# Three layer norms: the first token group finished from PSUM as the second one is, and the first tile's mean taken in a product bank

## The chip, the cores and the metric

The kernel runs on one core of a Trainium2 chip. The metric is device time in microseconds (us) of one execution; the time before is a median of three runs. The engines are named as in the profile: PE is TensorE, DVE is VectorE, ACT is ScalarE, POOL is GpSimd, SP issues the transfers. Each engine works its own queue strictly in order.

## The reference

Two trunk layers of a decoder run over 576 tokens (512 of a prompt, 64 of a sample), with D_MODEL = 1024. What matters here:

```python
def layer_norm(x, g, b):
    mu = jnp.mean(xf, -1, keepdims=True)
    var = jnp.mean(jnp.square(xf - mu), -1, keepdims=True)
    return ((xf - mu) * lax.rsqrt(var + LN_EPS)).astype(x.dtype) * g + b
...
        if l % 2 == 0:
            y, s1, wk1, r1 = ab_mixer(x, ...)
        else:
            y, c1 = conv_mixer(x, st_conv[i], w_in_conv[i], conv_w[i], w_out_conv[i])
        x = layer_norm(ALPHA * x + y, ln1_g[l], ln1_b[l])
        x = layer_norm(ALPHA * x + sqrelu_mlp(x, w_up[l], w_down[l]), ln2_g[l], ln2_b[l])
```

So there are four norms: norm 0 behind the first mixer, norm 1 behind the first MLP, norm 2 behind the conv mixer, norm 3 behind the second MLP, whose result is an output. The change is in the last three.

## The kernel before

**Layout.** Features lie on the partitions: x is eight tiles x0 to x7 of 128 features by 576 tokens. Tokens are cut into two groups, g0 and g1, of 288. A product of one feature tile and one group accumulates in one PSUM bank of the pool for products (`acc`, 6 banks); sums and means have a pool of two banks (`misc`). Weights and activations are each split into a high and a low part of a shorter format (`wh`, `wl`; `hh0` and `hl0` to `hh7` and `hl7` for the eight hidden tiles; `he`, `le`, `ho`, `lo` and again `hh`, `hl` for tiles of x), so each of the eight feature tiles of a contraction takes three matmuls (L152): high by high, low by high, high by low weight, and one product takes 24. The casts are L77 on ACT (high part) and L78 on DVE (low part).

**Norms 1 to 3.** A product that ends a residual branch is added to x tile by tile: `ln_add` (L271) for tile m = 0 to 7 and each group. At m = 0 the tile is added (L280; at norm 2, where the addition scales x too, L278), a matmul with a constant matrix takes its column mean into a bank named `cps` (L282), ACT copies it (L284), and it is taken off all eight tiles, on GpSimd at norms 1 and 3 (L291), on DVE at norm 2 (L289, L291). Tiles 1 to 7 are added by L293; ACT squares each (L296). Sums of the tiles and of their squares gather on GpSimd and DVE (L309) into `ln` and end in PSUM banks `ps` and `pq` by matmuls with constants (L319): all eight in one such sum for g0; for g1 tiles 6 and 7 go to the matmul directly.

**The finish.** When tile 7 of a group is added, the mean (`ps`) and mean square (`pq`) become a mean and a scale, and each tile is normalized, scaled and split for the next product. For g1 that is `ln_end` (L349), which keeps both in PSUM and works in place: d (L354), L355, Ln and Exp on ACT (L357, L358), the mean off each tile (L359, eight), L361 to L363, scale (L368, eight), high part on ACT (L375), low part on DVE (L376), x itself on ACT (L377). For g0 it is the other part of `ln_finish` (L380): mean and scale are copied to SBUF, five of the eight multiplications by the scale (L406) are on GpSimd.

**Order.** In the last product of a branch (`tail=TL`, 5) tiles 0 to 2 are done for both groups in turn, then tiles 3 to 7 of g0, then those of g1: g0's finish runs while PE works on g1's last five tiles. The code gives no order between engines; the framework's scheduler simulates a timeline and from it fixes each engine's queue before the run. Thus bank pools and buffers decide what stands where in PE's queue. The last tiles that norms 1 and 3 wait for are hh6, hl6, hh7, hl7, made from `ta` and `tb` in the branch before (ACT L1743, L1744, casts L77, L78). Behind norm 2 GpSimd forms sums of tiles of x (`ts`, L1712) and sums of weight tiles (L123, `raw`).

Of the kernel before, what the change touches and what calls it, by code (L numbers as in the profile page):

```python
# [10 lines left out]
F32 = mybir.dt.float32  # L11
F32R = mybir.dt.float32r
AF = mybir.ActivationFunctionType
ALU = mybir.AluOpType
PSUM = bass.MemoryType.PSUM

P = 128
NT = 576
GN = 288
KT = 8  # L20
ALPHA = 4.0 ** 0.25
LN_EPS = 1e-5


class Trunk:
# [245 lines left out]
    def ln_add(self, st, m, g, r, a, first):  # L271

        nc, cf = self.nc, self.cfg[st['n'], g]
        V, G = nc.vector, nc.gpsimd
        st[g, m] = r
        if m == 0:
            if first:
                V.scalar_tensor_tensor(out=r, in0=r, scalar=ALPHA, in1=a, op0=ALU.mult, op1=ALU.add)  # L278
            else:
                V.tensor_tensor(out=r, in0=r, in1=a, op=ALU.add)  # L280
            ps = self.p_misc.tile([P, GN], F32, tag="misc", name="cps")
            nc.tensor.matmul(ps, lhsT=self.ones128, rhs=r, start=True, stop=True)  # L282
            c = self.ln_tile(st, g, 'c')
            nc.scalar.copy(c, ps)  # L284
            for x in range(KT):
                t = st['x'][x][:, g * GN:(g + 1) * GN]
                e = G if x in cf['pg'] else V
                if first and x:
                    V.scalar_tensor_tensor(out=t, in0=t, scalar=ALPHA, in1=c, op0=ALU.mult, op1=ALU.subtract)  # L289
                else:  # L290
                    e.tensor_tensor(out=t, in0=t, in1=c, op=ALU.subtract)  # L291
        else:
            V.tensor_tensor(out=r, in0=r, in1=a, op=ALU.add)  # L293
        self.ln_sum(st, 's', m, g, r, cf['ds'], cf['sv'])
        t = self.p_tmp.tile([P, GN], F32, tag="t", name="lt", bufs=self.tb)
        nc.scalar.activation(t, r, AF.Square)  # L296
        self.ln_sum(st, 'q', m, g, t, cf['dq'], cf['qv'])
# [48 lines left out]
            nc.scalar.activation(r, r, AF.Identity, bias=b)  # L346
            if g and m == self.gated - 2: self.gate = [x.ins, y.ins]

    def ln_end(self, st, par, out, last):  # L349

        nc, V, pt = self.nc, self.nc.vector, self.p_tmp
        mean, v = st[1, 's', 'ps'], st[1, 'q', 'ps']
        d, w0, w = [pt.tile([P, GN], F32, tag="t", name=n, bufs=self.tb) for n in ('d', 'w0', 'w')]
        nc.scalar.activation(d, mean, AF.Square)  # L354
        V.scalar_tensor_tensor(out=v, in0=v, scalar=LN_EPS, in1=d, op0=ALU.add, op1=ALU.subtract)  # L355
        with self.tc.issue_after(self.pre.ins):
            nc.scalar.activation(w0, v, AF.Ln)  # L357
        nc.scalar.activation(w, w0, AF.Exp, scale=-0.5)  # L358
        sub = lambda r: V.tensor_tensor(out=r, in0=r, in1=mean, op=ALU.subtract)  # L359
        for m in range(3): sub(st[1, m])  # L360
        V.scalar_tensor_tensor(out=w0, in0=w, scalar=-0.5, in1=w, op0=ALU.mult, op1=ALU.mult)  # L361
        V.tensor_tensor(out=v, in0=v, in1=w0, op=ALU.mult)
        V.scalar_tensor_tensor(out=v, in0=v, scalar=1.5, in1=w, op0=ALU.add, op1=ALU.mult)  # L363
        gam, bet = par
        for m in range(KT):
            r, b = st[1, m], bet[:, m:m + 1]
            if m > 2: sub(r)
            V.scalar_tensor_tensor(out=r, in0=r, scalar=gam[:, m:m + 1], in1=v, op0=ALU.mult, op1=ALU.mult)  # L368
            if last:
                if m in (3, 6): V.tensor_scalar(out=r, in0=r, scalar1=b, scalar2=None, op0=ALU.add)  # L370
                else: nc.scalar.activation(r, r, AF.Identity, bias=b)
                out(m, 1, r)
                continue
            hi, lo = out(m, 1)
            x = nc.scalar.activation(hi, r, AF.Identity, bias=b)  # L375
            y = V.scalar_tensor_tensor(out=lo, in0=r, scalar=b, in1=hi.bitcast(F32), op0=ALU.add, op1=ALU.subtract)  # L376
            nc.scalar.activation(r, r, AF.Identity, bias=b)  # L377
            if m == self.gated - 2: self.gate = [x.ins, y.ins]

    def ln_finish(self, st, g, par, out, last=False):  # L380
        if g: return self.ln_end(st, par, out, last)
        nc = self.nc
        pt = self.p_tmp
        mean, e2 = st[g, 's', 'ps'], st[g, 'q', 'ps']
        mn = self.ln_tile(st, g, 'mn')
        nc.scalar.copy(mn, mean)
        d = pt.tile([P, GN], F32, tag="t", name="d", bufs=self.tb)
        nc.scalar.activation(d, mean, AF.Square)
        v = self.ln_tile(st, g, 'v')
        nc.vector.scalar_tensor_tensor(out=v, in0=e2, scalar=LN_EPS, in1=d, op0=ALU.add, op1=ALU.subtract)  # L390
        w0 = pt.tile([P, GN], F32, tag="t", name="w0", bufs=self.tb)
        with self.tc.issue_after(self.pre.ins):
            nc.scalar.activation(w0, v, AF.Ln)
        w = pt.tile([P, GN], F32, tag="t", name="w", bufs=self.tb)
        y = nc.scalar.activation(w, w0, AF.Exp, scale=-0.5)
        nc.vector.tensor_tensor(out=w0, in0=w, in1=w, op=ALU.mult)
        nc.vector.scalar_tensor_tensor(out=v, in0=v, scalar=-0.5, in1=w0, op0=ALU.mult, op1=ALU.mult)
        z = nc.vector.scalar_tensor_tensor(out=v, in0=v, scalar=1.5, in1=w, op0=ALU.add, op1=ALU.mult)
        if self.gated == 1 and g: self.gate = [z.ins, y.ins]
        gam, bet = par  # L400
        cf = self.cfg[st['n'], g]
        for m in range(KT):
            r = st[g, m]
            u = pt.tile([P, GN], F32, tag="t", name="u", bufs=self.tb)
            nc.vector.tensor_tensor(out=u, in0=r, in1=mn, op=ALU.subtract)  # L405
            (nc.vector if m in cf['mulv'] else nc.gpsimd).tensor_tensor(out=u, in0=u, in1=v, op=ALU.mult)  # L406
            def affine(e, o):
                if e is nc.scalar:
                    return e.activation(o, u, AF.Identity, scale=gam[:, m:m + 1], bias=bet[:, m:m + 1])
                return e.tensor_scalar(out=o, in0=u, scalar1=gam[:, m:m + 1], scalar2=bet[:, m:m + 1], op0=ALU.mult, op1=ALU.add)  # L410
            if last:
                affine(nc.vector if m in cf['affv'] else nc.scalar, r)
                out(m, g, r)
            else:
                dst = out(m, g)
                if self.direct:
                    a = affine(nc.scalar, dst[0])
                    affine(nc.vector, r)
                    b = nc.vector.tensor_tensor(out=dst[1], in0=r, in1=dst[0].bitcast(F32), op=ALU.subtract)
                    self.last = [a.ins, b.ins]  # L420
                else:
                    affine(nc.scalar, r)
                    self.parts(*dst, r)
            if self.gated >= 2 and g and m == self.gated - 2: self.gate = [x for x in self.last]


I32 = mybir.dt.int32
# [1437 lines left out]
```

## Time and profile before

| | |
|---|---|
| runs | 1532.83, 1533.28, 1534.14 us; median 1533.28 us |
| profiled execution | 1534.75 us, of which the traced span is 1533.0 us |
| PE, matmuls | 1465.6 us busy, 96% of the span |
| DVE | 1043.6 us, 68% |
| ACT | 647.4 us, 42% |
| GpSimd | 495.0 us, 32% |
| mean granted TensorE clock | 0.985 |

Times in rows of the trace are from the span's start. A row gives start, duration, engine, line, operation, tile written and tiles read, and in brackets how long the engine was idle before it and which engine's work ended that. The durations of matmuls overlap: at full clock one starts every 0.133 us though each shows 0.3 us. "x2" behind a row says that two like instructions are told together.

### The profile page before, as it was taken

The numbers are of one execution on the slowest core, as the hardware profiler recorded it, in microseconds if no ns is written. First come the engines' busy times: TensorE is split into PE (matmuls) and PEld (weight loads), VectorE is DVE, ScalarE is ACT, GpSimd is POOL, SyncE is SP. The second block draws the span as 40 slices with busy tenths as digits, with TensorE's granted clock in tenths as the row PEclk, the third lists the DMA queues.
The fourth block names the chain that finished last, engine by engine and source line by source line (L and its number), as shares of the span: only waits on it lengthen the run. The fifth ranks groups of instructions, "written<-read, shape, count | busy, mean of one in ns | idle before, by whom it ended". The sixth has DMA issues, their size and how long they took to land. (4 is left out here: it accounts for less than half of the span.)

```text
span 1533.0 us, 29786 instructions
## 1 busy us (share of the span) xinstructions
PE 1465.6 (96%) x11812; PEld 1416.3 (92%) x11812; DVE 1043.6 (68%) x2019; ACT 647.4 (42%) x1365; POOL 495.0 (32%) x554
## 2 busy tenths in 40 slices
PE   6999999999998999999999999899998999999996
PEld 5998898988787989999999998899998999999996
DVE  3565675876766984755747769788799475574755
ACT  3433433233333851533515435444366253351533
POOL 2032203356542331312213556332544131121354
PEclk9999999999999999999999999999999999999998
DMA  5332333535313042231422402223303223132221
GB/s 165 94 110 85 98 98 111 161 118 168 94 59 106 1 124 69 83 111 56 124 70 84 139 14 69 70 95 115 109 1 124 70 84 110 56 124 69 84 69 63
DMA packets 70940, 140.04 MB, mean 91 GB/s; under 512 B 21488, under 2 KB 30944, under 8 KB 70800
## 3 DMA queue, kind: packets, MB, share of 16 engines
q1 hardware_dynamic: 67968, 129.69, 27.3%
q0 software_dynamic: 1536, 5.57, 1.1%
q10 hardware_dynamic: 1296, 2.86, 0.6%
q8 instruction: 93, 1.52, 0.4%
q14 instruction: 47, 0.39, 0.1%
HBM read 124.39 MB, written 13.70 MB: 90 GB/s over the span
## 5 line engine op out<-in xcount | busy, mean ns | idle before, releaser
L77 ACT CAST wh<-raw 128x512 fp32r<-128x512 f32 x440 | 252.7, 618 | 409.1 <-PE acc L152 276.3
L78 DVE TENSOR_TENSOR wl<-raw,wh 128x512 fp32r<-128x512 f32 x440 | 325.9, 773 | 50.9 <-ACT wh L77 44.0
L152 PE MATMUL acc<-hh,wl 128*128 128x288 f32 x1180 | 348.7, 297 | 0.0
L152 PE MATMUL acc<-hl,wh 128*128 128x288 f32 x1180 | 348.1, 296 | 0.0
L152 PE MATMUL acc<-hh,wh 128*128 128x288 f32 x1180 | 345.7, 297 | 0.0
L152 PEld LDWEIGHTS acc<-hl,wh 128*128 128x128 f32 x1180 | 221.7, 188 | 0.5
L152 PEld LDWEIGHTS acc<-hh,wl 128*128 128x128 f32 x1180 | 221.6, 188 | 0.5
L152 PEld LDWEIGHTS acc<-hh,wh 128*128 128x128 f32 x1180 | 220.6, 188 | 0.3
L152 PE MATMUL acc<-xh,wh 128*128 128x288 f32 x480 | 148.3, 310 | 16.3 <-ACT xh L1541 13.3
L152 PE MATMUL acc<-ht,wh 128*128 128x288 f32 x444 | 133.0, 301 | 14.5 <-ACT s L244 6.1
L152 PE MATMUL acc<-xl,wh 128*128 128x288 f32 x480 | 146.2, 305 | 0.0
L152 PE MATMUL acc<-xh,wl 128*128 128x288 f32 x480 | 146.1, 304 | 0.0
L123 POOL TENSOR_TENSOR s<-raw 128x512 f32<-128x512 f32 x37 | 52.7, 1423 | 281.5 <-DMA raw<-in_w 210.8
L152 PE MATMUL acc<-lt,wh 128*128 128x288 f32 x444 | 132.4, 299 | 3.8 <-DVE lt L78 3.8
L152 PE MATMUL acc<-ht,wl 128*128 128x288 f32 x444 | 131.7, 298 | 0.0
L123 POOL TENSOR_TENSOR raw<-raw 128x512 f32<-128x512 f32 x37 | 57.2, 1545 | 164.2 <-DVE raw L123 110.0
L152 PEld LDWEIGHTS acc<-xh,wh 128*128 128x128 f32 x480 | 91.4, 191 | 19.8 <-ACT xh L1541 13.7
L152 PE MATMUL acc<-ho,wh 128*128 128x288 f32 x352 | 104.9, 298 | 0.0
L152 PE MATMUL acc<-lo,wh 128*128 128x288 f32 x352 | 104.5, 298 | 0.0
L152 PE MATMUL acc<-ho,wl 128*128 128x288 f32 x352 | 104.0, 298 | 0.0
L152 PEld LDWEIGHTS acc<-ht,wh 128*128 128x128 f32 x444 | 85.0, 192 | 16.4 <-ACT s L244 6.4
L152 PEld LDWEIGHTS acc<-xl,wh 128*128 128x128 f32 x480 | 91.5, 191 | 2.5 <-DVE xl L1542 0.7
(516 smaller groups left out, 3409.3 us busy)
## 6 DMA issues: line engine op xcount, KB each, us to landing
raw<-in_w SPq DMA_DIRECT2D x160, 512.0 KB, 3.8
raw<-in_w SPq DMA_DIRECT2D x60, 256.0 KB, 2.9
la<-in_w SPq DMA_DIRECT2D x32, 128.0 KB, 2.4
A<-stg SPq DMA_DIRECT2D x9, 288.0 KB, 3.2
x<-in_x POOLq DMA_DIRECT2D x8, 288.0 KB, 7.4
out_y<-x SPq DMA_DIRECT2D x16, 144.0 KB, 1.8
kr<-A SPq DMA_DIRECT2D x6, 288.0 KB, 2.6
lr<-in_x ACTq DMA_DIRECT2D x4, 288.0 KB
```

Source lines behind the costliest of these rows:

```text
L77: a = self.nc.scalar.copy(hi[:, s], src[:, s])
L78: b = self.nc.vector.tensor_tensor(out=lo[:, s], in0=src[:, s], in1=hi[:, s].bitcast(F32), op=ALU.subtract)
L123: tt = lambda e, o, x, y, op: e.tensor_tensor(out=o, in0=x, in1=y, op=op)
L152: mm = lambda w, x, a, b: self.nc.tensor.matmul(acc, lhsT=w, rhs=x, start=a, stop=b, skip_group_check=onto)
```

## The change

The column mean of m = 0 (`cps`) takes a bank of the product pool, for both groups of the three norms. `ln_end` becomes the only finish, for g0 too; the other part is gone. The copy of the mean, the multiplications on GpSimd and on DVE into `u`, and the temporary tiles go; for g0 there come eight L359, eight L368, eight L375, L376 and L377 (at norm 3 the last two kinds are replaced by the affine end). Behind the changed place the lines of the new kernel have smaller numbers: L1712 becomes L1666.

```diff
-            ps = self.p_misc.tile([P, GN], F32, tag="misc", name="cps")
+            ps = self.p_acc.tile([P, GN], F32, tag="acc", name="cps")
...
-    def ln_end(self, st, par, out, last):
+    def ln_finish(self, st, g, par, out, last=False):
...
-        mean, v = st[1, 's', 'ps'], st[1, 'q', 'ps']
+        mean, v = st[g, 's', 'ps'], st[g, 'q', 'ps']
...
-        for m in range(3): sub(st[1, m])
+        for m in range(3): sub(st[g, m])
...
-    def ln_finish(self, st, g, par, out, last=False):
-        if g: return self.ln_end(st, par, out, last)
...
-        mn = self.ln_tile(st, g, 'mn')
-        nc.scalar.copy(mn, mean)
...
-            nc.vector.tensor_tensor(out=u, in0=r, in1=mn, op=ALU.subtract)
-            (nc.vector if m in cf['mulv'] else nc.gpsimd).tensor_tensor(out=u, in0=u, in1=v, op=ALU.mult)
...
-                    affine(nc.scalar, r)
-                    self.parts(*dst, r)
```

The order of the queues moves at the following places. PE at norm 1, before: `acc_10122` is the product of m = 0, g0; `acc_10162` that of m = 0, g1; `acc_10210` and `acc_10241` those of m = 1.

```order
L152 MATMUL acc_10162<-hl3_6065,wh_9984 128x288
L152 MATMUL acc_10122<-hh6_6070,wh_9984 128x288
L152 MATMUL acc_10162<-hh3_6064,wl_9985 128x288
...
L152 MATMUL acc_10210<-hh1_6060,wh_9994 128x288
L152 MATMUL acc_10122<-hl6_6071,wh_9984 128x288
...
L152 MATMUL acc_10210<-hh4_6066,wh_9994 128x288
L152 MATMUL acc_10122<-hl7_6073,wh_9984 128x288
...
L152 MATMUL acc_10241<-hl3_6065,wh_9994 128x288
L282 MATMUL cps_10148<-x0_4548,o2_6036 128x288
L152 MATMUL acc_10241<-hh3_6064,wl_9995 128x288
L282 MATMUL cps_10188<-x0_4548,o2_6036 128x288
```

The same place now:

```order
L152 MATMUL acc_10122<-hh5_6068,wl_9985 128x288
L152 MATMUL acc_10122<-hh6_6070,wh_9984 128x288
L152 MATMUL acc_10122<-hl6_6071,wh_9984 128x288
L152 MATMUL acc_10122<-hh6_6070,wl_9985 128x288
L152 MATMUL acc_10122<-hh7_6072,wh_9984 128x288
L152 MATMUL acc_10122<-hl7_6073,wh_9984 128x288
L152 MATMUL acc_10122<-hh7_6072,wl_9985 128x288
L282 MATMUL cps_10148<-x0_4548,o2_6036 128x288
L152 MATMUL acc_10162<-hh0_6058,wh_9984 128x288
...
L152 MATMUL acc_10162<-hh7_6072,wl_9985 128x288
L282 MATMUL cps_10188<-x0_4548,o2_6036 128x288
```

The other products' matmuls no longer stand between those of the first product, and each mean stands directly behind its own product. It is so at norms 2 and 3 too; at norm 2 twelve matmuls of another sum (`acc<-ht`, `lt`) stand between hh5 and hh6, ahead of them 18 of the first product now and 24 matmuls before.

ACT at norm 2, before (`ta` and `tb` become hh6 and hh7):

```order
L77 CAST wh_12585<-raw_12375 128x512 x2
L77 CAST hh6_6070<-ta_12389 128x576
L77 CAST wh_12655<-raw_12383 128x512 x2
L77 CAST hh7_6072<-tb_12390 128x576
L77 CAST wh_12723<-raw_12499 128x512 x2
```

Now the same rows stand so:

```order
L77 CAST wh_12575<-raw_12365 128x512 x2
L77 CAST wh_12645<-raw_12373 128x512 x2
L77 CAST hh6_6070<-ta_12379 128x576
L77 CAST hh7_6072<-tb_12380 128x576
L284 COPY ln_12523<-cps_12521 128x288
```

The cast of hh6 has moved behind two casts of weights, and those of the next weights behind the first mean. DVE's low parts hl6 and hl7 have moved likewise, behind the two `wl` of those weights.

GpSimd behind norm 2, before:

```order
L1712 TENSOR_TENSOR ts_13478<-x4_4552 128x288
L1712 TENSOR_TENSOR ts_13459<-x1_4549,ts_13458 128x288
...
L1712 TENSOR_TENSOR ts_13469<-x3_4551,ts_13468 128x288
L1712 TENSOR_TENSOR ts_13489<-x7_4555,x6_4554 128x288
L123 TENSOR_TENSOR raw_12753<-raw_12753 128x4x128
L1712 TENSOR_TENSOR ts_13478<-x5_4553,ts_13478 128x288
```

And now:

```order
L1666 TENSOR_TENSOR ts_13448<-x3_4551,ts_13448 128x288
L1666 TENSOR_TENSOR ts_13458<-x4_4552 128x288
L123 TENSOR_TENSOR raw_12743<-raw_12743 128x4x128
L1666 TENSOR_TENSOR ts_13459<-x5_4553,x4_4552 128x288
...
L1666 TENSOR_TENSOR ts_13469<-x7_4555,x6_4554 128x288
L1666 TENSOR_TENSOR ts_13468<-x7_4555,ts_13468 128x288
```

The sum of weight tiles has moved from behind twelve of the sixteen `ts` to behind seven. In the finish of g1 at norms 1 and 2, L355 stood on DVE behind all eight L359 and stands behind the first of them; on PE the last matmul of the sums (`ps<-x7`) has moved four places back in both.

More of the change, by code (lines that the diff above doesn't have):

```diff
@@ L365, in ln_end @@
         for m in range(KT):
-            r, b = st[1, m], bet[:, m:m + 1]
+            r, b = st[g, m], bet[:, m:m + 1]
             if m > 2: sub(r)
@@ L371, in ln_end @@
                 else: nc.scalar.activation(r, r, AF.Identity, bias=b)
-                out(m, 1, r)
+                out(m, g, r)
                 continue
-            hi, lo = out(m, 1)
+            hi, lo = out(m, g)
             x = nc.scalar.activation(hi, r, AF.Identity, bias=b)
@@ L377, in ln_end @@
             nc.scalar.activation(r, r, AF.Identity, bias=b)
-            if m == self.gated - 2: self.gate = [x.ins, y.ins]
-    def ln_finish(self, st, g, par, out, last=False):
-        if g: return self.ln_end(st, par, out, last)
-        nc = self.nc
-        pt = self.p_tmp
-        mean, e2 = st[g, 's', 'ps'], st[g, 'q', 'ps']
-        mn = self.ln_tile(st, g, 'mn')
-        nc.scalar.copy(mn, mean)
[L387 to L404, printed above, removed]
-            nc.vector.tensor_tensor(out=u, in0=r, in1=mn, op=ALU.subtract)
[L406 to L421, printed above, removed]
-                    affine(nc.scalar, r)
-                    self.parts(*dst, r)
-            if self.gated >= 2 and g and m == self.gated - 2: self.gate = [x for x in self.last]
@@ L427 @@
+            if g and m == self.gated - 2: self.gate = [x.ins, y.ins]
 I32 = mybir.dt.int32
```

## The prediction

> **What bounds the kernel now.** I read the page first, then PE's longest waits, then the stretches around the three norms in the timeline, and last the order of both kernels.
>
> ```profile
> span 1533.0 us, 29786 instructions
> PE 1465.6 (96%) x11812; PEld 1416.3 (92%) x11812; DVE 1043.6 (68%) x2019; ACT 647.4 (42%) x1365; POOL 495.0 (32%) x554
> 1155.50 319.83 PE acc L152 x2387
> 892.50:911.00 18.50, 18.50 (x131) 17.82 (x130) 15.63 (x28) 10.31 (x25) 10.46 (x13) 1.00 0.00 1
> 850.00:892.00 42.00, 41.49 (x309) 41.04 (x307) 25.15 (x36) 16.32 (x33) 28.66 (x31) 1.00 0.33 102
> ```
>
> PE is busy for 96% of the span, and the third row, a piece of the chain that ended last, is 320 us of PE's products without a break. The last two rows are stretches of the view by windows: length, then busy time of PE, weight loads, DVE, ACT and GpSimd, the granted clock, transfers. 892.50 to 911.00 is g0's finish at norm 1: PE is busy in all of it. So work that the change takes off DVE, ACT and GpSimd in g0's finish is worth nothing there by itself; a change in what PE must wait for counts in full. 850 to 892 is where norm 1 begins, and PE loses half a microsecond there.
>
> **The removed work.**
>
> ```profile
> 898.20 3.84 POOL L406 TENSOR_TENSOR u<-u,ln 128x288 f32<-128x288 f32 x4 [0.46 <-DVE ln L398]
> 898.35 2.04 DVE L406 TENSOR_TENSOR u<-u,ln 128x288 f32<-128x288 f32 x2
> ```
>
> Per norm five multiplications leave GpSimd (3.84 us for four, so 4.8) and three leave DVE (1.02 each, 3.1); the copy of the mean leaves ACT. DVE gets no fewer passes beside them: a subtraction, a scale and a split per tile as before. I cost the shorter finish at 0: the cover is the 18.50 of 18.50 above, and g1's five products are as long as before. Were g0's parts late all the same, the next product's head would wait; DVE's lighter load speaks against it.
>
> **The first product of the norm.** The order puts the whole price on PE. These are the rows of norm 1.
>
> ```profile
> 851.45 0.29 PE L152 MATMUL acc<-hh,wh 128*128 128x288 f32 x1
> 853.71 0.30 PE L152 MATMUL acc<-hh,wl 128*128 128x288 f32 x1
> 855.34 0.76 DVE L78 TENSOR_TENSOR hl<-tb,hh 128x576 fp32r<-128x576 f32 x1 [0.52 <-issue]
> 859.17 0.30 PE L152 MATMUL acc<-hh,wl 128*128 128x288 f32 x1
> 859.50 0.82 DVE L280 TENSOR_TENSOR x<-x,acc 128x288 f32<-128x288 f32 x2 [3.41 <-PE acc L152]
> 862.50 0.65 PE L282 MATMUL cps<-x,o 128*128 128x288 f32 x2
> 1518.31 0.46 DVE L293 TENSOR_TENSOR x<-x,acc 128x288 f32<-128x288 f32 x1 [2.81 <-PE acc L152]
> ```
>
> The first 18 matmuls (hh0 to hh5) start from 851.45 to 853.71, 0.133 apart. hl7, the last input, is ready at 855.34 + 0.76 = 856.10. Before, other products' matmuls filled that time. Now the 18 are followed by hh6, hl6, hh7, hl7 of the same product, and nothing else may pass. Without a wait its 24th matmul would start at 851.45 + 23 x 0.133 = 854.51; now hl7's starts at 856.13 and the last 0.13 behind it, 856.26: **+1.75**. Then the mean. It needs the addition on DVE, which starts 0.33 behind the product's last matmul (859.17 to 859.50) and takes 0.46 (an addition of the same form, last row); with 0.05 for the signal, an estimate, PE starts the mean 0.84 behind instead of 0.13: **+0.71**. Before, the mean stood 3.0 us behind the addition's start (859.50, 862.50) and never waited. The second mean is the same: **+0.71**. Norm 1 together +3.17.
>
> Norm 3 has the same pattern:
>
> ```profile
> 1464.13 0.29 PE L152 MATMUL acc<-hh,wh 128*128 128x288 f32 x1
> 1468.01 0.76 DVE L78 TENSOR_TENSOR hl<-tb,hh 128x576 fp32r<-128x576 f32 x1 [0.50 <-issue]
> ```
>
> hl7 is ready at 1468.77, so the last matmul starts at 1468.94 against 1464.13 + 3.06 = 1467.19: +1.75, with the two means **+3.17**.
>
> Norm 2:
>
> ```profile
> 1064.25 0.30 PE L152 MATMUL acc<-hh,wh 128*128 128x288 f32 x1
> 1068.91 0.29 PE L152 MATMUL acc<-ht,wl 128*128 128x288 f32 x1
> 1067.94 0.68 ACT L77 CAST hh<-ta 128x576 fp32r<-128x576 f32 x1 [2.49 <-DVE ta L1794]
> 1069.15 1.14 ACT L77 CAST wh<-raw 128x512 fp32r<-128x512 f32 x2 [0.53 <-PE acc L152]
> 1071.48 0.75 DVE L78 TENSOR_TENSOR hl<-tb,hh 128x576 fp32r<-128x576 f32 x1
> 1080.95 1.19 DVE L289 SCALAR_TENSOR_TENSOR x<-x,ln 128x288 f32<-128x288 f32 x3
> ```
>
> The twelve `ht` matmuls now stand behind 18 matmuls instead of 24, so their last starts 0.80 earlier, 1068.11. The two casts of weights, which waited for it (1069.15), start at 1068.35 and end at 1069.49; hh6, now behind them, ends 0.63 later, 1070.12; hl6 follows on DVE, 1071.0; hl7 0.67 behind it, 1071.67. The product's last matmul starts at 1071.85 instead of 1068.91, the 36th start from 1064.25 on: **+2.94**. The first mean +0.71; the second +0.90, since eight subtractions (0.4 each by the L289 row) stand on DVE ahead of the second addition. Together +4.55.
>
> **What is given back.**
>
> ```profile
> 891.19 0.29 PE L152 MATMUL acc<-hh,wh 128*128 128x288 f32 x1
> 892.06 0.75 PE L319 MATMUL ps<-ln,o 128*128 128x288 f32 x2 [0.57 <-DVE ln L309]
> 863.66 14.88 POOL L291 TENSOR_TENSOR x<-x,ln 128x288 f32<-128x288 f32 x14 [13.03 <-ACT ln L284]
> 911.49 3.00 DVE L359 TENSOR_TENSOR x<-x,ps 128x288 f32<-128x288 f32 x8 [2.39 <-ACT d L354]
> 914.41 0.46 DVE L355 SCALAR_TENSOR_TENSOR pq<-pq,d 128x288 f32<-128x288 f32 x1
> 915.89 0.46 DVE L361 SCALAR_TENSOR_TENSOR w<-w 128x288 f32<-128x288 f32 x1 [1.01 <-ACT w L358]
> 1515.76 2.55 POOL L309 TENSOR_TENSOR ln<-ln,lt 128x288 f32<-128x288 f32 x3
> 1520.19 0.41 ACT L354 ACTIVATE d<-ps 128x288 f32<-128x288 f32 x1 [0.89 <-PE ps L319]
> ```
>
> At norm 1 the sum of g0 comes late to PE: it starts at 892.06, 0.87 behind the matmul ahead of it instead of 0.13 (0.73 lost). The sum hangs on GpSimd, whose 14 subtractions start when the first mean is copied, 863.66. The first mean now comes at 857.1, some 5.4 us earlier, while PE is 3.2 later: the wait goes, **-0.73**. In g1's finish (norms 1 and 2) L355 no longer waits for eight L359, so Ln and Exp run beside them, and L361 starts when L359 ends, 914.9 instead of 915.89: -1.05 with L355's own place; the last sum matmul stands four places later, +0.53; **-0.52** at each of the two. At the end, GpSimd's three sums (1515.76, until 1518.31) no longer have five multiplications among them, and d can start up to 0.34 earlier, as PE's last sums start right behind the last product: **-0.34**, between 0 and -0.5.
>
> Behind norm 2 PE waits long for a sum of weight tiles:
>
> ```profile
> 1150.75:1155.50 4.75, 0.29 (x3) 0.06 (x1) 4.33 (x5) 2.85 (x7) 4.75 (x5) 0.91 0.00 0
> 1154.60:1161.50 6.90, 6.00 (x25) 6.00 (x26) 6.90 (x9) 5.73 (x12) 4.57 (x5) 0.51 0.25 79
> 1153.02 1.78 POOL L123 TENSOR_TENSOR raw<-raw 128x512 f32<-128x512 f32 x1
> 1154.83 2.18 ACT L77 CAST wh<-raw 128x512 fp32r<-128x512 f32 x4 [0.46 <-POOL raw L123]
> ```
>
> PE stands for 4.62 us (4.75 less one pace), then runs at half clock for 25 matmuls, 6.00 busy for 25, 0.24 each instead of 0.133, 2.7 lost. The `raw` row moves five `ts` (1.0 to 1.3 each) forward, so this wait goes. But DVE is full in both windows (4.33 of 4.75, 6.90 of 6.90), with the same low parts to make ahead of PE's last matmuls there, and two more operations on weights now ahead of the last of them. So most of the time is waited for a little later, on DVE. The ends are 0 (DVE ends it all) and -7.3 (both lost pieces back); I take **-1.5**, near DVE's end, as DVE's rows have no idle time to give.
>
> **The clock.**
>
> ```profile
> 919.10:922.50 3.40, 1.46 (x7) 0.99 (x8) 3.40 (x9) 3.40 (x8) 0.00 (x0) 1.00 0.01 2
> 922.50:926.00 3.50, 3.50 (x16) 3.50 (x17) 3.50 (x8) 3.50 (x9) 0.39 (x1) 0.51 0.24 19
> 1027.00:1030.40 3.40, 1.29 (x10) 1.06 (x9) 1.89 (x3) 3.40 (x7) 0.00 (x0) 1.00 0.21 27
> ```
>
> A stretch of 3.4 us with 1.46 busy was followed by half clock for another 3.4; one with 1.29 busy (third row, clock 1.00 also behind it) was not, so it also hangs on where the stretch begins. At norm 2 PE has about 1.0 busy in the 4.35 us from 1068.25 on: half clock is likely there, at two in three by the share of beginnings of a 3.4 us window that are under 40% busy; cost 3.4 / 2 less the waits that hide some, **+1.5**, between 0 and 3.4. At norms 1 and 3 some 0.75 of 3.2 us is busy, one in three each: not taken, +1.5 each in the range.
>
> The Trainium skill, "TensorE: Matmul & The Clock Gate", Part 1, says that a free-running monitor of 3.4 us windows halves the clock after at least one idle window. Read strictly it gives no drop in any of the three places, since none is idle for a whole window, and the sum would be 7.3 instead of 8.8. The first two rows above speak against the strict reading: the 1.46 busy did not save the clock.
>
> **The sum.** Norm 1: 3.17 - 0.73 - 0.52 = 1.92. Norm 2: 4.55 - 0.52 - 1.5 = 2.53. Norm 3: 3.17 - 0.34 = 2.83. Together 7.28, with the clock at norm 2 8.8. The profiled execution took 1534.75 (its span 1533.0 and 1.75 around it), so 1543.5 in its terms; it stands 1.47 above the median of the runs, 1533.28, to which I add: **1542.0 us**.
>
> **Rivals.** (a) As summed, clock down at norm 2: 1542.0, own range 1540 to 1544. (b) The clock holds at all three, by the 1.29 row: 1540.5. (c) It falls at all three and nothing is gained behind norm 2: 8.8 + 3.0 + 1.5 = 13.3, 1546.6; for it speaks that the idle time lies within one window each, against it that windows must fall right three times. (d) Both pieces behind norm 2 come back, for which the moved `raw` speaks and DVE's full rows against: 8.8 - 5.8 = 3.0, and 1.5 without the clock, 1534.8 to 1536.3. At the lower end the change's losses are nearly paid and it does nothing one can measure. (e) The other side: the stretch behind norm 1 is bound by DVE.
>
> ```profile
> 935.00:960.00 25.00, 21.56 (x163) 21.33 (x161) 25.00 (x34) 10.19 (x19) 18.60 (x20) 1.00 0.12 43
> 959.90:963.30 3.40, 0.61 (x2) 0.61 (x3) 2.90 (x8) 2.86 (x7) 0.94 (x1) 0.53 0.00 0
> 963.30:966.70 3.40, 3.40 (x16) 3.40 (x15) 0.59 (x1) 1.60 (x4) 0.07 (x1) 0.50 0.52 154
> ```
>
> PE lost 3.4 before 960 and 2.8 behind it, and the clock stays at half through the third row too, 1.7 more: 7.9 in all. If GpSimd's freed time lets DVE's operations run faster there and all this goes, together with (d), the sum is 3.0 - 7.9 = -4.9: 1528.4. It takes (d) to get there: alone, 8.8 - 7.9 = +0.9 is no change. It decides from 8.8 given back in all. Against it: DVE has 25.00 of 25.00 to do, the change takes nothing from it between 922 and 960, and GpSimd's freed work lies before 907.
>
> **How the numbers follow.** Chances: (a) 0.38, (b) 0.22, (c) 0.14, (d) 0.16, (e) 0.06, something unseen 0.04. The range reaches from (d)'s upper end over (c), 1535.8 to 1546.8. A measurement tells 0.2%, 3.1 us, from no change. (a), (b), (c) and a third of (d) are slower; most of (d) is within it; (e) is faster: slower 0.82, same 0.12, faster 0.06.
>
> **What would show it.** In the changed kernel's timeline PE should stand before hl6 and hl7 at the three places with DVE's L78 as the releaser, and twice before `cps`, released by DVE's L280 or L278, 0.6 to 0.9 idle each; the view of waits should list `cps` L282, which it doesn't now. The mean granted clock should fall below 0.985 only if (a) or (c) holds. The wait for wh at 1150.75 should be gone, with others on `lt` in its place. I am wrong if PE starts `cps` without a wait, if the wait on hl7 is under 1 us, or if the stretch 922 to 963 gets shorter.

## The result

The changed kernel takes 1548.8 us (median of 4 runs, 1545.5 to 1551.5) against 1533.05 before (4 runs, 1528.5 to 1534.1): ratio 1.010 (1.0081 to 1.0119). In a second series it was 1550.9 against 1532.7, ratio 1.0117 (1.0097 to 1.0136). It is slower, as forecast, by 12 to 21 us (the two intervals) instead of 8.8, outside the range. The profiled execution of the changed kernel took 1547.8 us, 13.05 more than the one of before; its span is 1545.6.

The page of the changed kernel and its waits of PE (engine, operation, what it waited for: us in total, times, longest):

```profile
span 1545.6 us, 29782 instructions
PE 1480.0 (96%) x11812; PEld 1427.3 (92%) x11812; DVE 1039.2 (67%) x2036; ACT 647.0 (42%) x1360; POOL 478.5 (31%) x539
```

```profile
PE acc L152 <- DVE lt L78: 6.8, 4, 2.7
PE acc L152 <- ACT hh L77: 2.7, 3, 1.7
PE cps L282 <- DVE x L280: 2.3, 4, 0.6
PE acc L152 <- DVE hl L78: 1.6, 4, 0.5
PE cps L282 <- DVE x L278: 1.1, 2, 0.5
PE acc L152 <- ACT wh L77: 0.7, 1, 0.7
```

DVE, ACT and GpSimd have less to do than before, and PE more (1480.0 for 1465.6) with the same 11,812 matmuls: its busy share is 96% in both, so the page alone doesn't show the loss as idle time. The extra busy time is for the most part the clock, since a matmul's row is longer at half clock: half-clock time in the span goes from 47 to 78 us, and 20.5 of the 31 more lie ahead of 833 us, outside the change. The six waits on `cps` and the waits on hh of L77 and hl of L78 are new. The timeline of PE at norm 1:

```profile
853.90 0.29 PE L152 MATMUL acc<-hh,wh 128*128 128x288 f32 x1
854.33 0.40 PE L152 MATMUL acc<-hl,wh 128*128 128x288 f32 x1
854.57 0.29 PE L152 MATMUL acc<-hh,wl 128*128 128x288 f32 x1
855.36 0.40 PE L152 MATMUL acc<-hh,wh 128*128 128x288 f32 x1 [0.50 <-ACT hh L77]
856.21 0.40 PE L152 MATMUL acc<-hl,wh 128*128 128x288 f32 x1 [0.45 <-DVE hl L78]
856.45 0.29 PE L152 MATMUL acc<-hh,wl 128*128 128x288 f32 x1
857.37 0.72 PE L282 MATMUL cps<-x,o 128*128 128x288 f32 x2 [0.64 <-DVE x L280]
861.84 0.75 PE L282 MATMUL cps<-x,o 128*128 128x288 f32 x2 [0.55 <-DVE x L280]
```

One product's last six matmuls start from 853.90 to 856.45, and each mean waits for its addition. At norm 2 the same, and then the clock (windows, columns as in the prediction):

```profile
1070.90:1074.80 3.90, 1.68 (x11) 1.20 (x9) 3.26 (x6) 2.29 (x4) 0.00 (x0) 1.00 0.54 150
1074.80:1081.60 6.80, 6.25 (x23) 5.42 (x22) 3.64 (x10) 0.84 (x2) 0.00 (x0) 0.50 0.19 69
1033.80:1037.20 3.40, 3.40 (x16) 3.40 (x15) 3.40 (x6) 0.45 (x2) 1.75 (x1) 0.50 0.62 208
```

PE stands for most of 3.9 us and then runs 6.8 us at half clock, two windows and not one.

**Where the time went.** PE starts 11,812 matmuls in every one of these kernels, so the n-th start of a trace can be set beside the n-th of before. The difference of the two times, set to zero at 833 us, ahead of norm 1, is how far PE has fallen behind. Up to there the code is the same in all kernels of the table, and still PE gets there at anything between 827.6 and 836.9 us in profiles of that code, so this measure is sharper than the runs' times. Steps between points (times of before):

| stage | predicted | changed | again | bank only | finish only |
|---|---|---|---|---|---|
| norm 1, m = 0 (852 to 870) | +3.17 | +3.56 | +5.14 | +3.56 | 0.00 |
| g0's sums (to 894) | -0.73 | -0.84 | -0.84 | -0.84 | +0.25 |
| g1's finish (to 935) | -0.52 | -0.53 | -0.76 | -0.25 | -0.53 |
| conv mixer (to 1061) | 0 | +1.07 | +1.76 | -0.06 | +0.26 |
| norm 2, m = 0 (to 1082) | +4.55, clock +1.5 | +7.31 | +6.90 | +5.96 | 0.00 |
| g1's finish (to 1137) | -0.52 | -0.50 | -0.49 | 0.00 | -0.49 |
| behind it (to 1171, 1460) | -1.5 | -0.66 | +0.84 | -0.80 | -0.60 |
| norm 3, m = 0 (to 1479) | +3.17 | +3.52 | +4.85 | +5.06 | 0.00 |
| the end (to 1520) | -0.34 | -0.36 | -0.36 | +0.15 | -0.36 |
| sum | +8.8 | +12.6 | +17.0 | +12.8 | -1.5 |

In the changed kernel the three steps at m = 0 add up to 14.4; all else together gives back 1.8.

### The profile page after: what moved, and what is told of

Its sections match the earlier page's. It is cut to its first block, busy times and chain, and to the rows that moved or that the text cites. A ratio compares the mean times of both kernels' runs of the same rounds, so it can differ in the third digit from the quotient of the medians.

```text
span 1545.6 us, 29782 instructions
## 1 busy us (share of the span) xinstructions
PE 1480.0 (96%) x11812; PEld 1427.3 (92%) x11812; DVE 1039.2 (67%) x2036; ACT 647.0 (42%) x1360; POOL 478.5 (31%) x539
## 3 DMA queue, kind: packets, MB, share of 16 engines
q10 hardware_dynamic: 1296, 2.86, 0.6%
## 5 line engine op out<-in xcount | busy, mean ns | idle before, releaser
L77 ACT CAST wh<-raw 128x512 fp32r<-128x512 f32 x440 | 252.9, 618 | 407.7 <-PE acc L152 280.5
L78 DVE TENSOR_TENSOR wl<-raw,wh 128x512 fp32r<-128x512 f32 x440 | 326.9, 775 | 47.0 <-ACT wh L77 39.8
```

The costliest lines, as they stand in the source:

```text
L77: a = self.nc.scalar.copy(hi[:, s], src[:, s])
L78: b = self.nc.vector.tensor_tensor(out=lo[:, s], in0=src[:, s], in1=hi[:, s].bitcast(F32), op=ALU.subtract)
```

## The experiments

Theory: the mean's place in the product pool sets PE's order at m = 0, and that order is the loss. Rival: g0's new finish is the loss, since it holds two banks through sixteen passes. The column "again" and the two on the right are runs below.

**The bank alone** (kernel of before):

```diff
-            ps = self.p_misc.tile([P, GN], F32, tag="misc", name="cps")
+            ps = self.p_acc.tile([P, GN], F32, tag="acc", name="cps")
```

> Only the mean's bank moves to the product pool (three norms, both groups); g0 keeps the former finish. Order theory (the loss is PE's new order at the three m = 0 places): about as slow as the changed kernel, +10 to +15 us; PE's starts, matched one by one with those of before, fall behind by 3.5 at norm 1, 6 to 7.5 at norm 2, 3.5 at norm 3, and the long wait at 1150.75 stays, since the sum of weight tiles keeps its place. Finish theory (the loss is the new finish of g0, which holds the banks of mean and square through 16 passes): within 3 us of before.

Measured: 1548.6 us, ratio 1.0107 (1.0081 to 1.0133). PE falls behind by 3.56, 5.96 and 5.06 at the three places. One line is the whole loss. Its PE waits list the same rows as the changed kernel's, and the wait for weights behind norm 2 is still there:

```profile
PE acc L152 <- ACT wh L77: 5.2, 2, 4.5
PE cps L282 <- DVE x L280: 2.3, 4, 0.6
PE cps L282 <- DVE x L278: 1.1, 2, 0.5
```

At norm 3 it lost 1.54 more than the changed kernel, with the clock:

```profile
1474.20:1477.60 3.40, 3.38 (x12) 3.09 (x13) 0.46 (x1) 0.84 (x2) 1.54 (x2) 0.50 0.17 70
```

**The finish alone** (changed kernel, mean back in the pool of two banks: the line above the other way round).

> Only g0's finish from PSUM; the mean stays in the pool of two banks. Order theory: no loss at m = 0, so 0.5 to 3 us faster than before: 0.5 at each of norms 1 and 2 from g1's earlier scale, about 0.8 from the wait behind norm 2, up to 0.4 at the end. Finish theory: 10 us or more slower, with PE waiting for banks in g0's or g1's sums.

Measured: 1530.4 us, ratio 0.9986 (0.997 to 1.0002). No step at m = 0 (0.00 three times), no wait on `cps`; the gains of the finish are those in the table, 1.5 us in all, too little for the runs to tell from none. The rival falls.

**Norm 2 alone:**

```diff
-            ps = self.p_acc.tile([P, GN], F32, tag="acc", name="cps")
+            ps = self.p_acc.tile([P, GN], F32, tag="acc", name="cps") if st["n"] == 2 else self.p_misc.tile([P, GN], F32, tag="misc", name="cps")
```

> The changed kernel with the mean in the product pool at norm 2 alone; at norms 1 and 3 it is in the pool of two banks. Order theory: half the loss, PE falls behind at norm 2 alone by 4.5 (no half clock) to 7.5 (two windows of half clock), so the run is 3 to 7 us slower than before. Finish theory: as slow as the changed kernel.

Measured: 1538.6 us, ratio 1.0031 (1.0016 to 1.0046). PE falls behind by 6.18 at norm 2, with one window of half clock (from 1069.6), and by nothing at norms 1 and 3. The three places are separate.

**The product's own bank.** The addition has read the product when the mean is taken, so its bank is free:

```diff
-            ps = self.p_acc.tile([P, GN], F32, tag="acc", name="cps")
+            ps = a
```

> The changed kernel with the mean written into the product's own bank, which the addition has just read: no bank is taken from either pool for it. Order theory: PE's order is that of before at m = 0, so the same time as with the finish alone, 0.5 to 3 us faster than before. If instead any mean in a bank of the product pool costs, because the bank is held longer there: 3 us or more slower, with waits on L282 or on L152 for a bank. Finish theory: as slow as the changed kernel.

Measured: 1531.9 us, ratio 0.9984 (0.997 to 0.9998); no step at m = 0. So a mean in a product bank costs nothing by itself; an allocation of its own from that pool does.

**g0's mean alone, g1's alone.** `ps` is taken from the product pool for one group, from the pool of two banks for the other.

> The changed kernel with the mean in the product pool for g0 alone; g1's is in the pool of two banks. Order theory, with banks of the product pool given out in the order of the code: nothing may pass from the first product to its mean, so PE waits for hl6, hl7 and the first mean as in the changed kernel, but g1's mean stands a product behind its own and does not wait. PE falls behind by 2.5 to 3.0 at norms 1 and 3 (3.56 and 3.52 in the changed kernel) and by 3.7 to 6.5 at norm 2 (7.3). Rival, that the loss is the waits on the two means alone: 0.8 at each norm.

> The same with g1's mean alone in the product pool. Order theory: m = 0 of g1 may again stand between the pieces of m = 0 of g0, whose 24 matmuls cover the wait for hl7; only the products of m = 1 must wait until both means are placed. PE falls behind by 0.5 to 1.0 at norms 1 and 3 and by 0.5 to 2 at norm 2, so the run is within 2 us of before. Rival, that any mean in the product pool costs the same: half of the changed kernel's loss, 5 to 7 us.

Measured: g0 alone 1540.3 us, ratio 1.0046 (1.0031 to 1.0061); PE falls behind by 4.30 at norm 1 (one window at half clock in it, 1.5), 4.80 at norm 2, 2.71 at norm 3. g1 alone 1533.4 us, ratio 1.000 (0.9988 to 1.0012); 0.61, 1.25 and 0.54. The order of PE's queue with g1's mean alone, norm 1, the numbers and sizes left out:

```text
acc_10162<-hl3,wh
acc_10122<-hh6,wh
acc_10162<-hh3,wl
...
acc_10122<-hl7,wh
acc_10122<-hh7,wl
acc_10162<-hl7,wh
acc_10162<-hh7,wl
cps_10148<-x0,o2
cps_10188<-x0,o2
acc_10210<-hh0,wh
```

The two products of m = 0 are interleaved again and nothing of m = 1 (`acc_10210`) passes the means. With g0's alone nothing passes the first mean, and m = 1 passes the second. In all of these kernels, then, a product that the code opens behind a mean from the same pool stands behind that mean in PE's queue. Why the scheduler does so was not looked into further.

```profile
PE cps L282 <- DVE x L280: 0.7, 2, 0.4
PE acc L152 <- DVE hl L78: 0.4, 1, 0.4
PE cps L282 <- DVE x L278: 0.3, 1, 0.3
```

These are its waits: one per norm on `cps`, half as many as in the changed kernel, and one short one on hl. The rival that the waits on the means alone are the loss (0.8 a norm) falls by the run with g0's alone: without the second wait it still loses 2.7.

**The own bank with the former finish** (kernel of before, `ps = a`).

> The kernel of before with the mean written into the product's own bank; g0 keeps the former finish. Order theory: nothing moves at m = 0 and nothing is gained, within 1 us of before. If the gain of the two runs with the new finish came from the bank and not from the finish: 1.5 to 3 us faster.

Measured: 1534.6 us, ratio 1.000 (0.9986 to 1.0014); PE's starts end within 0.1 us of those of before. The small gain of the two runs with the new finish is the finish's.

**The changed kernel again.**

> The changed kernel once more, for its spread and a second profile. Order theory: PE falls behind by 3.5 at norm 1 and 3.5 at norm 3, or 1.3 to 1.5 more for each 3.4 us at half clock, and by 4.6 to 7.5 at norm 2; the median is 12 to 16 us above before. If the clock's share is chance, the half-clock stretches fall at other places than in the first profile; if it is fixed by the stalls, they fall at the same ones.

Measured: 1550.9 us (1546.7 to 1556.1, 6 runs), ratio 1.0117 (1.0097 to 1.0136); the median is 18.2 above before, past the 12 to 16 expected. Half clock falls at norms 1 and 3 as well now, and again for two windows at norm 2:

```profile
861.20:864.60 3.40, 3.40 (x12) 3.11 (x13) 0.46 (x1) 0.84 (x2) 1.62 (x2) 0.50 0.11 45
1485.80:1489.20 3.40, 2.90 (x10) 2.62 (x11) 0.90 (x2) 0.84 (x2) 1.06 (x2) 0.50 0.24 96
1079.60:1086.40 6.80, 5.75 (x21) 5.05 (x21) 3.96 (x10) 1.03 (x3) 0.00 (x0) 0.50 0.22 77
```

Against the first profile norm 1 costs 1.58 and norm 3 1.33 more, the price of a window. So where the clock falls is chance, but that it falls at m = 0 goes with the waits: in the profiles with g0's mean in the product pool it fell at norm 2 in four of five, at norms 1 and 3 in two of four each, and in the other nine profiles at none of the three places.

**Behind norm 2.** The wait of 4.62 on `raw` is gone in every kernel with the new finish, but PE gets at most 0.6 or 0.7 us of it back. Even that isn't shown to be the wait's: with the bank alone and with the own bank and the former finish the wait is still there, and PE gains 0.8 and 0.6 in the same stretch over the profile of before, in which two windows of half clock fall at the wait (from 1154.7) and not one. With the own bank and the new finish:

```profile
1138.00:1158.00 20.00, 17.20 (x114) 16.53 (x114) 19.81 (x19) 13.14 (x29) 18.44 (x16) 0.91 0.17 54
1140.83 1.06 DVE L376 SCALAR_TENSOR_TENSOR lo<-x,par,ho 128x288 fp32r<-128x288 f32 x1
1145.84 4.96 DVE L78 TENSOR_TENSOR wl<-raw,wh 128x512 fp32r<-128x512 f32 x4
1155.70 1.36 DVE L78 TENSOR_TENSOR lt<-ts,ht 128x576 fp32r<-128x576 f32 x1
```

DVE is busy for 19.81 of 20, GpSimd for 18.44. Three runs tell what fills DVE. First, less of its own work:

```diff
+            c = slice(0, 8 if g and m > 2 and st['n'] == 2 else GN)
-            y = V.scalar_tensor_tensor(out=lo, in0=r, scalar=b, in1=hi.bitcast(F32), op0=ALU.add, op1=ALU.subtract)
+            y = V.scalar_tensor_tensor(out=lo[:, c], in0=r[:, c], scalar=b, in1=hi.bitcast(F32)[:, c], op0=ALU.add, op1=ALU.subtract)
```

> The kernel with the mean in the product's own bank and the new finish; in g1's finish at norm 2 the low parts of tiles 3 to 7 (L376 on DVE, 1.05 us each) are computed for 8 of 288 columns only, which leaves most of that part of the output undone. Theory that DVE binds the stretch behind norm 2: some 4.5 us of DVE's work gone, PE's wait for lt there (2.7 us) shrinks or goes, and PE is 2 to 4.5 us earlier from 1171 on than in the run without the cut. Rival, that GpSimd's chain of differences binds it: DVE only waits longer for its inputs, PE gains under 1 us.

Measured: 1532.2 us, ratio 0.9994 (0.9982 to 1.0006). At 1171 PE is 0.7 earlier than with the whole low parts, and 1.2 from 1182 on; with the whole ones a window of half clock falls in the stretch (from 1153.6), here none. That is nearer to the rival's expectation, but the short low parts did not take away what they were meant to (L376 is L377 here):

```profile
1142.31 0.82 POOL L1667 TENSOR_TENSOR ts<-x 128x288 f32<-128x288 f32 x1
1142.31 0.83 DVE L377 SCALAR_TENSOR_TENSOR lo<-x,par,ho 128x8 fp32r<-128x8 f32 x1
1144.36 0.76 DVE L377 SCALAR_TENSOR_TENSOR hl<-x,par,hh 128x8 fp32r<-128x8 f32 x1
```

With 8 columns instead of 288 the operation still takes 0.8 us of 1.06. The time isn't its elements: the first of the two DVE rows lasts as long as the GpSimd row that starts with it. Inconclusive on its own; it points at GpSimd, which was at work beside it. So next the differences `ts` go to DVE:

```diff
-SUMV = ()
+SUMV = (0, 1, 2, 3)
```

> The same kernel (own bank, new finish) with all sixteen differences ts of a sequence on DVE instead of GpSimd, behind norms 1 and 2. DVE's operations on SBUF take 1.0 to 1.4 us while GpSimd works and 0.45 to 0.75 otherwise. Theory that sharing with GpSimd makes DVE the bound: 16 x 0.45 = 7.2 us come to DVE and some 10 go, so PE is 2 to 4 us earlier behind norm 2 and as much behind norm 1: 3 to 8 us faster than before. Rival, that DVE is full by its own work: 3 to 10 us slower.

> The same with half of the differences (the first two of each four) on DVE. Sharing theory: in between, or no gain at all, as GpSimd still works through most of the stretch: within 2 us of the run with none moved. Rival, DVE full by its own work: half the loss, 1.5 to 5 us slower.

Measured: all on DVE 1514.5 us, ratio 0.9873 (0.9859 to 0.9887); half, `SUMV = (0, 1)`, 1522.7 us, 0.9918 (0.9903 to 0.9933). That is 18.8 and 10.7 us faster than before, where 3 to 8 were expected of all and something in between of half; the rival, slower in both, falls. With all of them on DVE, and below them a row of the own-bank run with none moved:

```profile
1126.60 0.52 DVE L376 SCALAR_TENSOR_TENSOR lo<-x,par,ho 128x288 fp32r<-128x288 f32 x1
1133.62 1.88 DVE L78 TENSOR_TENSOR wl<-raw,wh 128x512 fp32r<-128x512 f32 x3
1138.54 0.74 DVE L78 TENSOR_TENSOR lt<-ts,ht 128x576 fp32r<-128x576 f32 x1
L1666 DVE TENSOR_TENSOR ts<-x,x x12: 440/451/455, 525.1 to 1132.9; 128x288 f32<-128x288 f32 x12
```

```profile
L1666 POOL TENSOR_TENSOR ts<-x,x x12: 1020/1252/1326, 520.5 to 1147.8; 128x288 f32<-128x288 f32 x12
```

Each of DVE's operations on SBUF takes about half as long (0.52 for 1.06, 0.63 for 1.24, 0.74 for 1.36), and a difference that took 1.25 us on GpSimd (median) takes 0.45. The first row of that kind stood in the prediction already: L406 takes 1.02 on DVE beside GpSimd. Beside the own-bank run PE gains 8.2 behind norm 1 (to 997) and 4.5 behind norm 2 (1137 to 1171), and some 6 more ahead of 833, where the same differences stand behind norm 0 (505 to 554), a place that the expectation left out. The Trainium skill, "SBUF — State Buffer", section "SBUF: two separate sides", says that DVE and GpSimd share a pair of SBUF ports as an exclusive lock, which a DVE operation with two SBUF inputs needs against a GpSimd operation that reads SBUF. The 8-column rows agree: the wait is for the other engine's operation, not for a share of bandwidth. So does the one slow low part in the run with all differences on DVE:

```profile
1127.86 1.46 POOL L123 TENSOR_TENSOR raw<-raw 128x512 f32<-128x512 f32 x1 [26.93 <-ACT hh L77]
1128.06 1.57 DVE L376 SCALAR_TENSOR_TENSOR lo<-x,par,ho 128x288 fp32r<-128x288 f32 x1
```

It takes 1.57 instead of 0.52 and ends 0.3 behind the only operation of GpSimd there. The rows that read a PSUM bank and one SBUF tile agree too: L206 takes 0.44 to 0.46 in both kernels, also at 1152.96 in the own-bank run, while GpSimd is at work.

**Without the change** (kernel of before, all differences on DVE):

> The kernel of before (mean in the pool of two banks, former finish of g0) with all sixteen differences on DVE. If the gain of the run before last came from the sharing of DVE and GpSimd behind norms 1 and 2 alone, it is here as well: 15 to 20 us faster than before, and the new finish adds 0 to 3. If the new finish is needed for it, since it frees GpSimd or DVE earlier: less than 10 us.

Measured: 1518.4 us, ratio 0.9903 (0.9887 to 0.992), 15.2 us faster. Most of the gain needs nothing of the change. What the finish and the own bank add, 3.9 us between the medians of two series and not 0 to 3, lies behind norm 2: PE gains 5.1 there (14.62 to 19.73 us ahead of before) and 1.5 without (14.91 to 16.38). The fastest version is the one with the own bank, the new finish and all differences on DVE: 1514.5 us.

## Why the prediction was right in its direction and too low

- **The order at m = 0** is the loss, shown by the bank alone. Taken at 3.17, 4.55 and 3.17; without half clock 3.56 at norm 1 (0.4 above), 5.06 at norm 2 (an estimate: 7.31 less 21 matmuls at 0.107 more each), 3.52 at norm 3. The mis-sized part is the pace behind a wait: the next matmul starts 0.24 behind one that waited, not 0.13 (854.33 and 854.57, 856.21 and 856.45 above), and at each place at least three such waits follow one another, for hl7 and the two means. The second mean at norm 2 was too dear: it waits 0.55 like the others, which is 0.71 and not 0.90 in all. One sign that was named against the prediction came true without telling against it: no wait on hl7 reaches 1 us. At norm 1 it is spread over three matmuls, 0.3 before hl6 (854.33, and not 0.13 behind 853.90), 0.50 before hh7, which ACT releases, and 0.45 before hl7.
- **The clock** is the step that failed. I took one window at norm 2, 1.5 us, and none elsewhere. The price of a window at norms 1 and 3 was right (1.3 to 1.6), the count was not: two windows at norm 2 in both profiles of the changed kernel, and one at each of norms 1 and 3 half of the time, where I had one in three. In the runs of the second series the mean granted clock is 0.977 on average and 0.982 before: 35 us of the span lost to it instead of 28, so up to 7 of the 18 us are the clock's, an estimate and an upper bound, since a lost clock costs nothing where PE waits. The 40% by which I counted the chance is no measured limit: the prediction's own rows have half clock behind 1.46 busy of 3.40 and none behind 1.29. Why two windows came at norm 2 isn't shown. In both profiles the wait for the first mean (until 1076.40 in the first) lies inside the first of them, and PE is busy there for 2.86 and 2.36 of 3.41 us; with the bank alone and at norm 2 alone it is 2.92 and 3.40, and one window came. The wait for the second mean (1083.26) lies behind both.
- **The conv mixer**, 0, measured +1.07 and +1.76. A window of half clock falls at 1033.80 in the first profile and 4.9 later in the second, but the step isn't shown to belong to the change: the same window falls with the bank alone and with the own bank too, where the stage costs -0.06 and -0.05, since it ends in a wait of PE on `u` (0.69 at 1053.27 before) that takes the loss up. In the one profile of before it did not fall.
- **In sum**, the first profile passes the forecast 8.8 by 3.8: 1.25 from m = 0 without half clock, 0.75 from the clock at norm 2, 1.07 from the conv mixer, 0.84 from behind norm 2, -0.1 from the rest. In the second the windows at norms 1 and 3 add 2.9 more. The medians are 15.7 and 18.2 above before; what of this no profile shows stays open. The Trainium skill's rule ("TensorE: Matmul & The Clock Gate", Part 1), read strictly, rival (b), gives no drop here; both profiles have drops behind windows in which PE worked part of the time, 1.68 of 3.90 at 1070.90.
- **g0's sum at norm 1**, -0.73, was right (-0.84), for the reason given: the bank alone has it too and the finish alone has not. **g1's finish**, -0.52, was right at both norms and belongs to the finish. **The end**, -0.34, measured -0.36.
- **Behind norm 2**, -1.5: -0.66 and, with another fall of the clock, +0.84. The wait did come back on `lt`, as forecast (2.7 us), and the -0.66 isn't shown to be the moved `raw`'s. DVE was the bound, but not by its own work, as I had argued from its full rows: about half of the time of its operations on SBUF was a wait on GpSimd.
- **g0's shorter finish at 0** was right where PE was covered: nothing is lost or gained between 894 and 914 in any profile.
- Rival (e), the stretch behind norm 1: no step there, as argued. But its price was real: moving the differences took 8.2 us from it. My working looked there only for GpSimd's freed time before 907, not for GpSimd's work in the stretch itself.

## What to carry to other kernels

With a scheduler like this one a pool of banks also orders the queue of the engine that fills them: in these kernels no product opened behind a mean from the same pool passed that mean, and an extra bank for a small sum is better found in a tile just read. Before a unit is called full, see whether its operations of one shape all take the same time; two durations for one shape can be a wait inside the row, and moving work onto the "full" engine can then make it faster. Where new idle time comes in pieces close together, price the clock by all of them, with a chance for each place.

## What the hardware showed that was not expected

- One DVE operation on SBUF of 128x288 takes 0.44 to 0.52 us with GpSimd idle and 1.06 beside it, and 0.8 beside it with only 8 columns.
- The first matmul behind a wait sets the next back to 0.24 us, at full granted clock, where a stream has 0.133.
- The granted clock's falls differ from one execution to the next in the same code: half-clock time ahead of 833 us was 20 to 44 us in the profiles of that code. It is part of the spread between runs of one kernel: in the second series the changed kernel's slowest run, 1556.1 us, has a mean clock of 0.973, its fastest, 1546.7, 0.980. It isn't all of it: before, with 20.5 us of half clock ahead of 833, and the changed kernel, with 41.0, get there within 0.06 us of each other.
